# The modulation product with its weights as the stationary operand and two columns of conditions as the moving one

## The chip, the cores and the metric

The kernel runs on one core of one Trainium2 chip. The metric is the device time of one execution in microseconds (us). Three runs of the kernel before gave 1486.37, 1487.2 and 1495.71 us; the median is 1487.2 us.

## The reference, cut to what matters

The program is one inference step with two layers over 128 context tokens and 1024 latent tokens. Each layer begins with a modulation: a conditioning vector (one for the latent tokens, one for the context tokens) goes through SiLU and through a linear map, and gives a shift, a scale and a gate of 1024 values each.

```
mod = jax.nn.silu(cond) @ w_mod + b_mod               # w_mod: (1024, 3072) per layer, float32
shift, scale, gate = jnp.split(mod, 3, axis=-1)
h = _rmsnorm(x, g_pre) * (1.0 + scale[:, None, :]) + shift[:, None, :]
z = h @ w_in                                          # feeds attention, a gating MLP and a DeltaNet
...
return x + gate[:, None, :] * _rmsnorm(mix, g_post)   # mix = concatenated branches @ w_out
```

So the product has two rows of conditions, 1024 inputs and 3072 outputs, and its weights are 12 MB per layer. The scale and the shift are wanted by all that follows in their layer; the gate is wanted only by the layer's end.

## The kernel before

Tokens are in nine tiles of 128 (t = 0 to 7 latent, t = 8 context). A normalised tile is transposed on TensorE, scaled and shifted per feature, and split into two float16 halves, X (`make_h`, L275 to L291). Every projection of X (`proj_tok`, L165 to L171) is three float16 products per 128 inputs.

The order of the program is this. In the **prologue** (L1081 to L1102) the scale and the shift of layer 0 are made (parts 1 and 0 of `mod`, four `next` calls, L1087), then nine tiles are loaded, normalised and turned into X. Both scale and shift are in the tile `AB`; nothing of X can be made before it. Then, for each layer, `merge` (L1104) interleaves a chain (the DeltaNet) with a filler (the gating MLP, then attention) by estimated costs that the generators yield. The attention generator calls `next(other)` once after each tile of heads (L1018); `other` is the rest of the modulations: the gate of layer 0 (part 2) and all three parts of layer 1. At last `out_layer` projects back, makes the X of the next layer, and takes the gate from DRAM (`gg_d`).

The instructions are put in their order on each engine ahead of time by a scheduler of the framework; each engine then runs its own list in that order and waits where an operand is missing. SyncE (SP) issues nearly all DMAs, those of the attention's transposes too (`turn`), from one list.

`mod` (L210 to L259) takes 512 output columns at a time. Four loads of 512 KB bring the weights: 256 inputs x 512 columns each, in runs of 2 KB (L245). In the prologue they have 16 buffers of their own (`wm`); later they share two staging buffers (`st`) with the loads of the projection weights. The conditions are the stationary operand: the tile `csp` has 8 blocks of 32 columns, of which two hold conditions and 30 hold zeros. The four matmuls of four input blocks write to four groups of 32 partitions, so the result is in four partial sums on 128 partitions (L249). They are copied to SBUF (L251), and `finish` adds the four and transposes at once by products with a selection matrix `selc` (L227, for scale and shift: stationary are 128x128 blocks of the copy, moving the two columns of `selc`), then adds the bias. For the gate (L220) the sums stay as rows, and bias and `g_post` are loaded as rows by two small DMAs (L217, L218).

In the profile one float32 matmul of this kind shows as two records of weight load and two of matmul: 96 matmuls of L249 are 192 records, 32 of L227 are 64.

Of the kernel before, what the change touches and what calls it, by code (L numbers as in the profile page):

```python
# [11 lines left out]
F32 = mybir.dt.float32  # L12
# [34 lines left out]
def hybrid_trunk(  # L47
# [145 lines left out]
    def silu_cond(mp_):  # L193
# [10 lines left out]
        csp = mp_.tile([128, 8, 32], F32, name="csp")  # L204
        G.memset(csp, 0.0)
        V.scalar_tensor_tensor(csp[:, :, 0:2].transpose([0, 2, 1]), th.rearrange("p (c k) -> p c k", c=2), 1.0,
# [3 lines left out]
    def mod(l, vt, mp_, csp, AB, wmp=None):  # L210
        mt = [mp_.tile([128, 8, 2], F32, tag=f"mt{i}", name=nm("mt")) for i in range(2)]

        def finish(part, cb, mp):
            f0 = 4 * (cb % 2)
            if part == 2:
                rows = stg.tile([128, 4, 256], F32, tag="st", name=nm("gr")).rearrange("p a b -> p (a b)")[0:2].rearrange("p (a c) -> p a c", a=2)
                dma(rows[:, 0], b_mod[l, 512 * cb:512 * cb + 512].partition_broadcast(2))  # L217
                dma(rows[:, 1], g_post[l, 128 * f0:128 * f0 + 512].partition_broadcast(2))  # L218
                pm = bank("o", 1)
                T.matmul(pm[0:2, :], selc, mp, start=True, stop=True)  # L220
                V.tensor_tensor(rows[:, 0], pm[0:2, :], rows[:, 0], op=ALU.add)
                V.tensor_tensor(rows[:, 0], rows[:, 0], rows[:, 1], op=ALU.mult)
                dma(gg_d[l][:, 128 * f0:128 * f0 + 512], rows[:, 0])
                return
            pm = bank("o", 1)
            for b in range(4):
                T.matmul(pm[:, 2 * b:2 * b + 2], mp[:, 128 * b:128 * b + 128], selc, start=True, stop=True)  # L227
            V.tensor_tensor(mt[part][:, f0:f0 + 4], pm[:, 0:8].rearrange("p (f c) -> p f c", c=2),
                            bc(vt[:, 16 + 8 * part + f0:20 + 8 * part + f0], 2, 2), op=ALU.add)
            if cb % 2 and part == 1:  # L230
                V.scalar_tensor_tensor(AB[:, 0], mt[1], 1.0, bc(vt[:, 0:8], 2, 2), op0=ALU.add, op1=ALU.mult)
            elif cb % 2:
                V.tensor_copy(AB[:, 1], mt[0])

        todo = []
        for part in (1, 0, 2):
            for cb in (2 * part, 2 * part + 1):
                ps = psp()
                for k2 in range(4):
                    if wmp is not None and part < 2:  # L240
                        st = wmp.tile([128, 4, 256], F32, tag="wm", name=nm("wm"), bufs=16)
                    else:
                        st = stg.tile([128, 4, 256], F32, tag="st", name=nm("st"))
                    s = st.rearrange("p a b -> p (a b)").rearrange("p (k c) -> p k c", k=2)
# [5 lines left out]
                mp = mp_.tile([128, 512], F32, tag="mp", name=nm("mp"), bufs=2 if PIPE else 1)  # L250
                (V.tensor_copy if wmp is not None and part < 2 else S_.copy)(mp, ps)  # L251
                todo.append((part, cb, mp))
                if len(todo) > PIPE:
                    finish(*todo.pop(0))
# [1000 lines left out]
```

## Time and profile before

| | |
|---|---|
| time of the profiled execution | 1490.02 us |
| its span | 1487.9 us |
| median of three runs | 1487.2 us |
| busy share of the span: TensorE matmul, weight load | 88%, 68% |
| VectorE, ScalarE, GpSimd | 65%, 44%, 44% |
| mean granted TensorE clock | 0.945 of full |

A busy matmul engine is not one at its peak: matmuls are pipelined, and a record lasts longer than the distance to the next one. The cost of a stream of matmuls is read from the distances of starts. The granted clock has two levels, 1.0 (2.4 GHz) and 0.5 (1.2 GHz); a value between is a mean over both.

### The profile page before, as it was taken

Reading aid. Unit: us, or ns where it says so; the run is one execution under the profiler, and the core shown is the slowest. Engines: PE = TensorE matmul, PEld = TensorE weight load, DVE = VectorE, ACT = ScalarE, POOL = GpSimd, SP = SyncE. Lnnn points to the kernel's source line nnn. Section 1 sums busy time; section 2 is a strip of 40 time slices with the busy share of each in tenths; the row PEclk is TensorE's granted clock in tenths of the full one; section 3 lists DMA queues with packets and bytes.
Section 4 is the critical chain, followed back from the end, with each engine's and each line's share of the span. In section 5 each row is a group of like instructions: output and inputs, shape, how many; then the busy total and the mean of one; then the engine's idle time right before and its main releaser. Section 6 shows DMA issues by size and latency. Waiting matters only on the chain.

```text
span 1487.9 us, 37881 instructions
## 1 busy us (share of the span) xinstructions
PE 1311.8 (88%) x15191; PEld 1004.7 (68%) x15191; DVE 960.6 (65%) x2302; ACT 657.9 (44%) x1483; POOL 649.8 (44%) x890
## 2 busy tenths in 40 slices
PE   6899988899989699969998998889898769987997
PEld 2665566476668587758896655668676658865786
DVE  2865689986465684664446677797966375776333
ACT  2733545624465414742334344442567322765211
POOL 0751256624375423762223433553568512667200
PEclk9999999998999888989999998899999889998999
DMA  9331034727774225775342211332476111776553
GB/s 362 107 90 41 23 98 129 150 88 184 159 163 114 40 59 111 122 167 160 128 132 76 59 36 58 95 82 59 81 133 111 37 44 46 146 110 138 155 177 107
DMA packets 301563, 162.90 MB, mean 109 GB/s; under 512 B 212623, under 2 KB 277939, under 8 KB 301387
## 3 DMA queue, kind: packets, MB, share of 16 engines
q1 hardware_dynamic: 301261, 160.45, 44.2%
q8 instruction: 119, 1.95, 0.6%
q14 instruction: 58, 0.47, 0.1%
q10 hardware_dynamic: 125, 0.04, 0.0%
HBM read 95.78 MB, written 24.28 MB: 81 GB/s over the span
## 4 chain that ended last, share of the span: by engine, by line
PE 46%; DVE 18%; DMA 16%; issue 8%; POOL 7%; ACT 5%; SPq 1%; ACTq 0%; DVEq 0%; POOLq 0%
PE ps L170 13%; PE ps L1052 10%; PE ps L312 7%; DMA PT<-P 6%; DVE sv L500 2%; DVE sv L502 2%; POOL P L931 2%; PE ps L249 2%; PE ps L947 1%; DMA mix_d<-oc 1%; DMA st<-in_w_mod_dram 1%; PE ps L533 1%; DMA st<-in_w_in_dram 1%; PE ps L698 1%; PE ps L517 1%
## 5 line engine op out<-in xcount | busy, mean ns | idle before, releaser
L170 PEld LDWEIGHTS <-X 128*128 128x128 f16 x3888 | 351.8, 100 | 106.3 <-issue 42.0
L170 PE MATMUL ps<-wg,X 128*128 128x256 f16 x2592 | 330.5, 280 | 12.0 <-DVE wg L161 4.8
L931 POOL TENSOR_TENSOR P<-sS,P 128x512 f16<-128x512 f32 (+2 forms) x144 | 151.6, 1056 | 84.4 <-ACT sS L929 57.9
L1052 PEld LDWEIGHTS <-OTm 128*128 128x128 f16 x1728 | 169.7, 99 | 24.5 <-DMA OTm<-mix_d 2.6
L1052 PE MATMUL ps<-wo,OTm 128*128 128x256 f16 x1296 | 152.5, 277 | 1.9 <-DMA OTm<-mix_d 1.9
L312 PE MATMUL ps<-X,wg 128*128 128x512 f16 (+1 forms) x864 | 146.0, 328 | 1.8 <-ACT wg L160 1.4
L928 ACT ACTIVATE P<-sS,nmx 128x512 f16<-128x512 f32 (+2 forms) x144 | 94.3, 660 | 72.4 <-DVE nmx L926 46.5
L926 DVE CUSTOM_DVE_ANT_0 sS<-ps,am,nsk 128x512 f32<-128x512 f32 (+2 forms) x144 | 95.0, 669 | 42.1 <-PE ps L922 27.3
L312 PEld LDWEIGHTS <-wg 128*128 128x128 f16 x864 | 74.1, 99 | 68.5 <-ACT wg L160 1.8
L170 PE MATMUL ps<-wb,X 128*128 128x256 f16 x864 | 105.4, 284 | 11.6 <-ACT wb L160 6.6
L947 PE MATMUL ps<-Vt,PT 128*128 128x128 f16 (+1 forms) x992 | 71.4, 212 | 36.0 <-DMA PT<-P 34.9
L929 ACT ACTIVATE sS<-sS,nmx 128x512 f32<-128x512 f32 (+2 forms) x144 | 94.9, 659 | 4.6
L145 POOL TENSOR_TENSOR rs<-ms,mhalf 128x1 f32<-128x1 f32 x36 | 19.9, 554 | 168.9 <-DVE ms L1061 93.2
L947 PEld LDWEIGHTS <-PT 128*128 128x128 f16 x992 | 50.2, 100 | 55.0 <-DMA PT<-P 46.1
L319 DVE SCALAR_TENSOR_TENSOR y<-zT,cw,y 128x1156 f32<-128x1156 f32 x48 | 68.9, 1438 | 28.5 <-ACT y L317 27.9
L500 DVE TENSOR_TENSOR sv<-sv 128x31 f32<-128x31 f32 (+15 forms) x186 | 78.1, 420 | 3.8
L502 DVE TENSOR_TENSOR sv<-sv 128x31 f32<-128x31 f32 (+15 forms) x186 | 74.3, 399 | 4.0
L922 PE MATMUL ps<-KT,qT 128*128 128x128 f16 (+2 forms) x272 | 68.8, 267 | 0.0
L161 DVE SCALAR_TENSOR_TENSOR wg<-st,wg 128x1024 f16<-128x1024 f32 x44 | 55.4, 1268 | 19.4 <-ACT wg L160 19.2
L1055 ACT ACTIVATE sq<-ps 128x512 f32<-128x512 f32 x36 | 21.3, 594 | 100.8 <-PE ps L1052 57.8
L921 PE MATMUL ps<-KT,qT 128*128 128x128 f16 (+2 forms) x272 | 60.2, 268 | 6.0 <-DVE nmx L926 3.5
L160 ACT ACTIVATE wg<-st 128x1024 f16<-128x1024 f32 x44 | 45.3, 1055 | 43.3 <-DMA st<-in_w_in_dram 29.3
(271 smaller groups left out, 2818.0 us busy)
## 6 DMA issues: line engine op xcount, KB each, us to landing
st<-in_w_in_dram SPq DMA_DIRECT2D x40, 512.0 KB, 4.6
st<-in_w_mod_dram SPq DMA_DIRECT2D x32, 512.0 KB, 4.4
OTm<-mix_d SPq DMA_DIRECT2D x18, 512.0 KB, 4.9
wm<-in_w_mod_dram SPq DMA_DIRECT2D x16, 512.0 KB, 7.9
xt<-in_x_sample_dram SPq DMA_DIRECT2D x16, 512.0 KB, 11.8
st<-in_w_out_dram SPq DMA_DIRECT2D x16, 512.0 KB, 4.6
mix_d<-OTA SPq DMA_DIRECT2D x36, 128.0 KB, 3.3
xs<-xt SPq DMA_DIRECT2D x9, 512.0 KB
```

The source lines that it names most:

```text
L170: T.matmul(ps, X[:, t, k, a, :], wg[:, k, b, c0:c0 + n], start=(i == 0), stop=(i == 23))
L312: T.matmul(ps[:, 0:n], wg[:, k, b, 128 * hg:128 * hg + 128], X[:, t0:t1, k, a, :], start=(i == 0), stop=(i == 23))
L319: V.scalar_tensor_tensor(y, zT[:, tap:tap + 1156], cw[:, tap * 6 + ct:tap * 6 + ct + 1], y, op0=ALU.mult, op1=ALU.add)
L500: V.tensor_tensor(t3, m3[:, 0:m, m:m + 1].to_broadcast([128, m, w]), y3[:, m:m + 1, m:32].to_broadcast([128, m, w]), op=ALU.mult)
L502: V.tensor_tensor(y3[:, 0:m, m:32], y3[:, 0:m, m:32], t3, op=ALU.subtract)
L922: T.matmul(ps[:, cs], qT[:, h, :], Kl[:, kv, ks], start=False, stop=True)
L926: V.tensor_tensor_reduce(sS[:, 0:nk], ps[:, 0:nk], mk, -0.125, nsk[:, hh:hh + 1], ALU.add, ALU.min, accum_out=nmx[:, h:h + 1])
L928: S_.activation(P16[:, 0:nk], sS[:, 0:nk], AF.Exp, bias=nmx[:, h:h + 1], scale=-1.0)
L929: S_.activation(sS[:, 0:nk], sS[:, 0:nk], AF.Exp, bias=nmx[:, h:h + 1], scale=-1.0, accum_out=sm[:, h:h + 1])
L931: G.tensor_tensor(P16[:, nk:2 * nk], sS[:, 0:nk], P16[:, 0:nk], op=ALU.subtract)
L947: T.matmul(pops[:, 128 * h:128 * h + n], PT[:, a * nb + j, :], Vt[:, blist[j], kv].rearrange("p s d -> p (s d)")[:, 0:n], start=(i == 0), ...
L1052: T.matmul(ps[:, 256 * i:256 * i + 256], OTm[:, k, a, :], w[:, k, b, :], start=(n == 0), stop=(n == 23))
```

## The change

`csp` is now 128x8x2, without zeros. A new function `block(part, f, ws)` makes 128 outputs at once: eight matmuls, over eight blocks of 128 inputs, with a 128x128 block of the weights as the stationary operand and `csp[:, k, :]`, two columns, as the moving one. They are added up in one of the three `psp` banks, which the projections use too. The result is features by conditions already: ScalarE adds the bias of scale and shift on its way out of PSUM (128x2), VectorE adds the bias of the gate and multiplies by `g_post`. The copy, the products with `selc` and the small loads are gone; the gate is turned into rows by one transpose per layer. In the prologue the loads stay as they were. Elsewhere a load of 512 KB now brings all 1024 inputs of 128 columns, in runs of 512 B, and one `next` makes two blocks from two loads, where it made 512 columns from four; the 8 calls that found work are now 16, of 18 places. The cost yielded to the interleaving was 3.5 for each of 8 calls, and is 1.8 for each of 16.

```
-        csp = mp_.tile([128, 8, 32], F32, name="csp")
-        G.memset(csp, 0.0)
+        csp = mp_.tile([128, 8, 2], F32, name="csp")
...
+        def block(part, f, ws):
+            ps = psp()
+            for k in range(8):
+                T.matmul(ps[:, 0:2], ws[k], csp[:, k, :], start=(k == 0), stop=(k == 7))
+            bias = vt[:, 16 + 8 * part + f:17 + 8 * part + f]
             if part == 2:
...
+                V.tensor_scalar(mt[2][:, f, :], ps[:, 0:2], bias, vt[:, 8 + f:9 + f], op0=ALU.add, op1=ALU.mult)
+            else:
+                S_.activation(mt[part][:, f, :], ps[:, 0:2], AF.Identity, bias=bias)
+
+        def finish(part):
+            if part == 2:
                 pm = bank("o", 1)
...
+                T.transpose(pm[0:16, 0:128], mt[2].rearrange("p f c -> p (f c)"), ident)
+                rows = mp_.tile([16, 128], F32, tag="gr", name=nm("gr"))
+                V.tensor_copy(rows, pm[0:16, 0:128])
+                dma(gg_d[l].rearrange("c (f q) -> f c q", q=128), rows)
...
         for part in (1, 0, 2):
-            for cb in (2 * part, 2 * part + 1):
-                ps = psp()
-                for k2 in range(4):
...
-                    dma(s, w_mod[l, 256 * k2:256 * k2 + 256, 512 * cb:512 * cb + 512].rearrange("(k p) c -> p k c", p=128))
-                    for kk in range(2):
-                        k = 2 * k2 + kk
-                        j = k % 4
-                        T.matmul(ps[32 * j:32 * j + 32, :], csp[:, k, :], s[:, kk, :], start=(k < 4), stop=(k >= 4))
...
+            if wmp is not None and part < 2:
+                for cb in range(2):
+                    ws = [None] * 8
+                    for k2 in range(4):
+                        st = wmp.tile([128, 2, 512], F32, tag="wm", name=nm("wm"), bufs=16)
+                        dma(st, w_mod[l, 256 * k2:256 * k2 + 256, 1024 * part + 512 * cb:1024 * part + 512 * cb + 512]
+                            .rearrange("(k p) c -> p k c", p=128))
+                        ws[2 * k2], ws[2 * k2 + 1] = st[:, 0], st[:, 1]
+                    for b in range(4):
+                        block(part, 4 * cb + b, [w[:, 128 * b:128 * b + 128] for w in ws])
...
+                    yield 3.6
+                continue
+            for f in range(8):
+                st = stg.tile([128, 4, 256], F32, tag="st", name=nm("st"))
+                s = st.rearrange("p a b -> p (a b)").rearrange("p (k c) -> p k c", k=8)
+                dma(s, w_mod[l, :, 1024 * part + 128 * f:1024 * part + 128 * f + 128].rearrange("(k p) c -> p k c", p=128))
+                block(part, f, [s[:, k, :] for k in range(8)])
...
+                if f % 2:
+                    yield 1.8
```

How the change moves instructions is shown at three places; a number behind a name is that of a buffer.

TensorE in the prologue, before: the first 512 columns and their `finish` (`wm` are the weight tiles, `csp` the conditions, the moving operand stands first).

```order
L249 MATMUL ps_137<-wm_138,csp 32x512 x2
L249 MATMUL ps_137<-wm_142,csp 32x512 x2
L249 MATMUL ps_137<-wm_146,csp 32x512 x2
L249 MATMUL ps_137<-wm_150,csp 32x512 x2
L227 MATMUL ps_156<-selc,mp_154 128x2 x4
```

The same place in the changed kernel (line numbers are its own).

```order
L216 MATMUL ps_145<-csp,wm_137 128x2 x2
L216 MATMUL ps_155<-csp,wm_137 128x2 x2
L216 MATMUL ps_165<-csp,wm_137 128x2 x2
L216 MATMUL ps_145<-csp,wm_139 128x2 x2
L216 MATMUL ps_155<-csp,wm_139 128x2 x2
L216 MATMUL ps_165<-csp,wm_139 128x2 x2
L216 MATMUL ps_145<-csp,wm_141 128x2 x2
L216 MATMUL ps_155<-csp,wm_141 128x2 x2
L216 MATMUL ps_165<-csp,wm_141 128x2 x2
```

Three blocks run side by side as the weight tiles come in, in three banks; the fourth follows when a bank is free. In all there are 16 blocks, 128 such matmuls, with one other matmul (the transpose of the bias vectors) among them, ahead of the first transpose of a token tile.

ScalarE in the prologue, before: squares for the norms (L265), a conversion of projection weights (L160) and, sixth, the first use of `AB` (L286).

```order
L265 ACTIVATE sq_241,ss_242<-xt_239 128x1024
L265 ACTIVATE sq_251,ss_252<-xt_249 128x1024
L160 ACTIVATE wg_259<-st_260 128x4x256
L265 ACTIVATE sq_270,ss_271<-xt_268 128x1024
L265 ACTIVATE sq_303,ss_304<-xt_301 128x1024
L286 ACTIVATE hf_278<-ps_279,AB_125 128x128 x2
```

The same place in the changed kernel; L221 takes a block out of its bank.

```order
L160 ACTIVATE wg_351<-st_356 128x4x256
L221 ACTIVATE mt_134<-ps_252,vt_122 128x2
L221 ACTIVATE mt_134<-ps_262,vt_122 128x2
L160 ACTIVATE wg_1370<-st_1371 128x4x256
L221 ACTIVATE mt_134<-ps_272,vt_122 128x2
L160 ACTIVATE wg_1370<-st_1375 128x4x256
L221 ACTIVATE mt_134<-ps_290,vt_122 128x2
L221 ACTIVATE mt_134<-ps_300,vt_122 128x2
L221 ACTIVATE mt_134<-ps_310,vt_122 128x2
L221 ACTIVATE mt_134<-ps_320,vt_122 128x2
L264 ACTIVATE sq_395,ss_396<-xt_393 128x1024
L285 ACTIVATE hf_370<-ps_371,AB_124 128x128 x2
```

The blocks' way out of PSUM now stands among conversions of projection weights. Of the four conversions of the prologue, one stood ahead of the first use of `AB` before, and all four do now.

SyncE in the attention of layer 0, before (`PT` and `qT` are transposes that the heads wait for, `gr` the rows of the gate).

```order
L933 DMA_TRANSPOSE PT_3299<-P_448_3294 128x2x128
L217 DMA gr_3345<-in_b_mod_dram 2x512
L218 DMA gr_3345<-in_g_post_dram 2x512
L245 DMA st_3617<-in_w_mod_dram 128x2x512
L889 DMA rt_4242<-in_rope_dram 128x128
L933 DMA_TRANSPOSE PT_3310<-P_452_3305 128x2x128
L933 DMA_TRANSPOSE PT_3321<-P_456_3316 128x2x128
L245 DMA st_3621<-in_w_mod_dram 128x2x512
L899 DMA_TRANSPOSE qT_3464<-ql_3461 128x4x128
L933 DMA_TRANSPOSE PT_3545<-P_488_3540 128x6x128
L933 DMA_TRANSPOSE PT_3562<-P_492_3557 128x6x128
L245 DMA st_3625<-in_w_mod_dram 128x2x512
```

The same place in the changed kernel.

```order
L253 DMA st_3703<-in_w_mod_dram 128x8x128
L898 DMA_TRANSPOSE qT_3317<-ql_3314 128x4x128
L253 DMA st_3715<-in_w_mod_dram 128x8x128
L932 DMA_TRANSPOSE PT_3380<-P_449_3375 128x2x128
L932 DMA_TRANSPOSE PT_3391<-P_453_3386 128x2x128
L932 DMA_TRANSPOSE PT_3402<-P_457_3397 128x2x128
L932 DMA_TRANSPOSE PT_3413<-P_461_3408 128x2x128
L888 DMA rt_3982<-in_rope_dram 128x128
L253 DMA st_3907<-in_w_mod_dram 128x8x128
L932 DMA_TRANSPOSE PT_3634<-P_489_3629 128x6x128
L898 DMA_TRANSPOSE qT_3553<-ql_3550 128x4x128
L932 DMA_TRANSPOSE PT_3649<-P_493_3644 128x6x128
```

Of each `next` four loads through two buffers stood before among the transposes; now two loads stand there, and the small ones of the gate are gone.

## Rows read from the trace of the kernel before

**Rows 1.** Page, parts 1 and 4: engines; the chain that ended last, by engine.

```profile
PE 1311.8 (88%) x15191; PEld 1004.7 (68%) x15191; DVE 960.6 (65%) x2302; ACT 657.9 (44%) x1483; POOL 649.8 (44%) x890
PE 46%; DVE 18%; DMA 16%; issue 8%; POOL 7%; ACT 5%; SPq 1%; ACTq 0%; DVEq 0%; POOLq 0%
```

**Rows 2.** Busy us by stretch; columns named in the first row.

```profile
core 0: us, PE busy (x) PEld busy (x) DVE busy (x) ACT busy (x) POOL busy (x), PEclk, DMA share, GB/s
5.00:30.00 25.00, 19.77 (x98) 6.55 (x99) 4.96 (x15) 2.30 (x4) 0.55 (x1) 1.00 1.05 392
33.00:75.00 42.00, 34.06 (x272) 27.84 (x273) 35.40 (x84) 33.16 (x68) 28.99 (x34) 0.91 0.41 137
225.00:450.00 225.00, 202.61 (x2295) 138.88 (x2293) 169.82 (x439) 112.91 (x275) 116.54 (x164) 0.95 0.63 147
450.00:675.00 225.00, 190.10 (x2844) 157.88 (x2842) 141.72 (x383) 104.11 (x246) 109.77 (x164) 0.90 0.50 107
```

**Rows 3.** Timeline of the prologue: start us, us, what, [idle before it].

```profile
5.53 5.30 PE L249 MATMUL ps<-wm,csp 128*32 128x512 f32 x16 [2.50 <-DMA wm<-in_w_mod_dram]
...
11.62 0.97 PEld L227 LDWEIGHTS ps<-selc,mp 128*128 128x128 f32 x8 [1.91 <-DVE mp L251]
...
12.61 0.14 PEld L249 LDWEIGHTS ps<-wm,csp 128*32 128x32 f32 x2
...
27.62 1.05 PE L227 MATMUL ps<-selc,mp 128*128 128x2 f32 x8 [0.79 <-DVE mp L251]
...
29.78 0.17 DVE L233 COPY AB<-mt 128x16 f32<-128x16 f32 x1
...
33.33 1.68 DVE L288 TENSOR_SCALAR hf<-ps,AB 128x128 f32<-128x128 f32 x5
...
47.09 1.05 ACT L160 ACTIVATE wg<-st 128x1024 f16<-128x1024 f32 x1
```

**Rows 4.** Timeline of two streams of small matmuls and what followed one.

```profile
77.81 4.34 PE L170 MATMUL ps<-wab,X 128*128 128x16 f16 x167
...
358.42 4.34 PE L517 MATMUL ps<-sv,NA 32*32 32x32 f32 x128
362.69 1.87 PE L227 MATMUL ps<-selc,mp 128*128 128x2 f32 x8
364.48 1.92 PE L249 MATMUL ps<-st,csp 128*32 128x512 f32 x4
```

**Rows 5.** Stretches of these streams, matmul engine alone: busy, PEclk, DMA share, GB/s.

```profile
75.30:81.80 6.50, 6.50 (x225) 1.00 0.19 50
81.90:85.00 3.10, 3.10 (x54) 0.50 0.88 271
...
361.90:368.70 6.80, 6.80 (x42) 0.52 0.20 52
```

**Rows 6.** Groups by line and shape: busy us, mean ns, idle before, releaser.

```profile
L249 PE MATMUL ps<-st,csp 128*32 128x512 f32 x128 | 36.4, 633 | 5.8 <-DMA st<-in_w_mod_dram 5.8
...
L220 PE MATMUL ps<-mp,selc 128*2 128x512 f32 x8 | 4.1, 592 | 0.2 <-ACT mp L251 0.2
...
L161 DVE SCALAR_TENSOR_TENSOR wg<-st,wg 128x1024 f16<-128x1024 f32 x44 | 55.4, 1268 | 19.4 <-ACT wg L160 19.2
...
L958 ACT ACTIVATE es<-es 128x4 f32<-128x4 f32 x36 | 7.0, 194 | 0.2
```

**Rows 7.** Stretch 225 to 450, L227 alone: matmul, weight load, PEclk, DMA.

```profile
225.00:450.00 225.00, 4.98 (x32) 4.69 (x32) 0.95 0.63 147
```

**Rows 8.** The chain between 225 and 460, shares by line.

```profile
by line: PE ps L170 13.2%; PE ps L249 9.7%; DMA st<-in_w_mod_dram 9.0%; issue 8.6%; DVE sv L500 6.6%; DVE sv L502 5.9%; DMA PT<-P 4.1%; DVE sS L926 2.5%; PE ps L947 2.3%; PE ps L533 2.0%; DMA st<-in_w_in_dram 2.0%; PE ps L517 1.8%; PE ps L9
```

**Rows 9.** SP's waits: for whom, total us, times, longest.

```profile
SPq L245 <- PE ps L249: 21.3, 12, 6.7
```

**Rows 10.** DMA issues: KB each, median us to landing.

```profile
st<-in_w_mod_dram SPq DMA_DIRECT2D x32, 512.0 KB, 4.4
...
st<-in_w_in_dram SPq DMA_DIRECT2D x16, 256.0 KB, 3.1
```

More of the change, by code (lines that the diff above doesn't have):

```diff
@@ L203, in silu_cond @@
         V.tensor_scalar(ct, ct, 0.5, None, op0=ALU.mult)
[L204 to L206 removed]
+        csp = mp_.tile([128, 8, 2], F32, name="csp")
+        V.scalar_tensor_tensor(csp.transpose([0, 2, 1]), th.rearrange("p (c k) -> p c k", c=2), 1.0,
                                ct.rearrange("p (c k) -> p c k", c=2), op0=ALU.add, op1=ALU.mult)
@@ L210, in mod @@
     def mod(l, vt, mp_, csp, AB, wmp=None):
-        mt = [mp_.tile([128, 8, 2], F32, tag=f"mt{i}", name=nm("mt")) for i in range(2)]
-        def finish(part, cb, mp):
-            f0 = 4 * (cb % 2)
-            if part == 2:
-                rows = stg.tile([128, 4, 256], F32, tag="st", name=nm("gr")).rearrange("p a b -> p (a b)")[0:2].rearrange("p (a c) -> p a c", a=2)
-                dma(rows[:, 0], b_mod[l, 512 * cb:512 * cb + 512].partition_broadcast(2))
-                dma(rows[:, 1], g_post[l, 128 * f0:128 * f0 + 512].partition_broadcast(2))
-                pm = bank("o", 1)
[L220 to L230, printed above, removed]
@@ new lines, in mod @@
+        mt = [mp_.tile([128, 8, 2], F32, tag=f"mt{i}", name=nm("mt")) for i in range(3)]
+        def block(part, f, ws):
[3 more added lines that the diff above has]
+            bias = vt[:, 16 + 8 * part + f:17 + 8 * part + f]
+            if part == 2:
+                V.tensor_scalar(mt[2][:, f, :], ps[:, 0:2], bias, vt[:, 8 + f:9 + f], op0=ALU.add, op1=ALU.mult)
+            else:
+                S_.activation(mt[part][:, f, :], ps[:, 0:2], AF.Identity, bias=bias)
@@ L233, in finish @@
                 V.tensor_copy(AB[:, 1], mt[0])
-        todo = []
         for part in (1, 0, 2):
-            for cb in (2 * part, 2 * part + 1):
-                ps = psp()
-                for k2 in range(4):
[L240 to L244, printed above, removed]
-                    dma(s, w_mod[l, 256 * k2:256 * k2 + 256, 512 * cb:512 * cb + 512].rearrange("(k p) c -> p k c", p=128))
-                    for kk in range(2):
-                        k = 2 * k2 + kk
-                        j = k % 4
-                        T.matmul(ps[32 * j:32 * j + 32, :], csp[:, k, :], s[:, kk, :], start=(k < 4), stop=(k >= 4))
[L250 to L254, printed above, removed]
-                if (part, cb) in ((0, 1), (2, 5)):
-                    for x in todo:
-                        finish(*x)
-                    todo = []
-                yield 1
@@ new lines, in mod @@
+            if wmp is not None and part < 2:
[8 more added lines that the diff above has]
+                        block(part, 4 * cb + b, [w[:, 128 * b:128 * b + 128] for w in ws])
+                    if cb:
+                        finish(part)
+                    yield 3.6
+                continue
@@ new lines, in mod @@
+            for f in range(8):
[3 more added lines that the diff above has]
+                block(part, f, [s[:, k, :] for k in range(8)])
+                if f == 7:
+                    finish(part)
+                if f % 2:
+                    yield 1.8
@@ L1017, in attention @@
                             yield from heads(p2, prev, *ready.pop(0))
-                            if next(other, None) is not None:
-                                yield 3.5
+                            got = next(other, None)
+                            if got is not None:
+                                yield got
                     while pend:
```

3 lines of the change are left out of this document (2 added, 1 removed).

## The prediction, written before the changed kernel was run

> **What bounds the kernel now.** I read the page first, for the engines and the chain. TensorE is the busiest engine and holds nearly half of the chain that ended last [rows 1]. A change that gives or takes TensorE time therefore counts wherever TensorE is what the rest waits for, and there are two such places for the modulation.
>
> The first is the prologue. The stretch 5 to 30 us is bound by loads: 392 GB/s with the DMA engines fully busy, TensorE at 19.8 of 25 us [rows 2]. A weight tile of 512 KB comes each 1.34 us (0.524 MB over 392 GB/s), and TensorE follows it. The last product with `selc` starts at 27.62, the finished shift is in `AB` at 29.78 + 0.17 = 29.95, and its first use starts at 33.33 [rows 3]. From there to 75 the nine tiles are made, with VectorE busy 35.4 of 42 us [rows 2].
>
> The second is the attention of layer 0, from about 225 on, where the other 8 x 512 columns are made. Between 225 and 450 TensorE is busy 202.6 of 225 us, and 190.1 in the next 225 [rows 2]. The chain there gives L249 9.7% of 235 us = 22.8 us, and the waits for its weight loads 9.0% = 21 us [rows 8].
>
> **The price of a block.** The trace of before has the very instruction of the new blocks, a float32 128x128 stationary operand with two moving columns: L227. Eight records (four matmuls) at 11.62 are followed by the next weight load at 12.61 [rows 3], so a record takes 0.99/8 = 0.124 us, and a block of 16 records 1.98 us. The distance is that of the weight loads, which lie back to back. At the lower clock the same eight records start at 362.69 and the next matmul at 364.48 [rows 4], 1.79 us: 0.224 per record, 3.58 us per block.
>
> At 0.124, 48 blocks (16 in the prologue, 32 in the attention) cost 95 us. What they replace: in the attention L249 36.4 and L220 4.1 [rows 6] and L227 5.0 [rows 7], together 45.5 us; there 32 blocks cost 63.4. The zeros of the padded operand were cheap, since four partial products ran side by side on four groups of partitions; a weight load of 128 columns for two moving ones is dear.
>
> **Which clock the stream has.** In the prologue the 16 blocks are one stream of 256 records, with nothing wide among them. Two streams of small matmuls in the trace kept the engine fully busy and lost the clock. One with 16 moving columns and dense weight loads [rows 4] fills most of 75.3 to 81.8 at 1.00, and from 81.9 it is 0.50; the other, 128 records of 32x32, begins at 358.4, and 361.9 to 368.7 has 0.52, though TensorE is busy throughout [rows 5]. The matmuls of 512 columns in 5 to 30, with gaps, kept 1.00 [rows 2]. So I take the new stream to lose the clock about 5 us after its start, between the 3.5 and the 6.6 us of the two.
>
> **The sum, prologue.** The stream starts at 5.53 as before [rows 3]. It is no longer fed too slowly: three blocks side by side need 12 records x 0.124 = 1.49 us per weight tile, more than the 1.34 of its load. At 10.5, 20 of the 128 matmuls are done (0.248 each); the other 108 at 0.447 take 48.3 us, so it ends at 58.8 (57.5 to 60.0 for a loss at 12.1 or at 9.0). With the way out on ScalarE (nearest row, 128x4: 0.194 [rows 6]) and the copy, 0.17, the first use starts at about 59.6, 26.3 us later than 33.33. Some of it is caught up. By then all token tiles have landed and four conversions are done, three of which lay behind 33.33: 3 x 1.27 = 3.8 us of VectorE [rows 6]. VectorE also waits 42 - 35.4 = 6.6 us in that stretch. The catch-up lies between 0 and 10.4; I take 6, past the middle, since the loads no longer hold anything up while the chains between engines do. Prologue: **+20.3**, bounds +14 to +27.
>
> **The sum, attention.** TensorE has 63.4 - 45.5 = +17.9 at full clock. One of the four L227 groups in this stretch ran at the lower one [rows 4], so I take a quarter of the blocks at 3.58: 8 x 1.60 = +12.8, together +30.7 (bounds +17.9 and, all blocks low, +69). On the path lies the share that L249 has now, 22.8/36.4 = 0.6: +18.4. Against it stands the wait for the weights. A call issues two loads into two free buffers where four went through two, so the 5.8 us of TensorE's waits for them [rows 6], and SP's waits for L249, 21.3 us [rows 9] with the transposes queued behind, become less. I take 4. Attention: **+14.4**.
>
> Loads in runs of 512 B: the nearest row is 256 KB of projection weights in such runs, 3.1 us to landing, against 4.4 for 512 KB in runs of 2 KB [rows 10]; 512 KB then takes between 4.4 and 6.2. They are issued a call ahead, so I cost them at nothing; without that cover it is up to 32 x 1.8 = 58 us of landing time, 0.6 of it on the path. Of the 32 blocks' ways out, 16 are on ScalarE, 3.1 us, and 16 on VectorE about as much, on engines with half and a quarter of the stretch free [rows 2]: nothing. A block holds one of the three banks that the projections use; that is in the bounds.
>
> Together +34.7: 1490.0 + 34.7 = 1524.7 for an execution like the profiled one, which is 2.8 us above the median of the runs. Against the median: **1522 us**.
>
> **The rivals.**
>
> *The stream keeps its pace*: the clock holds, or the weight loads don't go with it. The stream would end at 5.5 + 31.7 = 37.2. But on ScalarE the blocks' ways out stand behind conversions whose loads come late: the third conversion starts at 47.09 now [rows 3], and the thirteenth block's way out stands behind the fourth. So the first use lies between 38 and 50, +5 to +16; at the middle, with 2 caught up, +8. The attention gives 17.9 x 0.6 - 4 = +7. Time 1487.2 + 15 = 1502. The two lost clocks [rows 5] and 1.79 us against 0.99 [rows 3, 4] speak against it. Chance 0.2. The Trainium skill, "TensorE: Matmul & The Clock Gate", section "LDWEIGHTS (loading the stationary operand)", has such a rule: a load takes its columns over 1.2 ns, at any clock. By that, 256 loads of 128 columns are an estimated 27.3 us and the stream ends at 32.9; the trace agrees at the full clock (0.124 against 0.107), and not at the lower (0.224).
>
> *The attention runs low too*: wide projections between the blocks don't hold the clock, and all 32 blocks cost 3.58. Then 69 x 0.6 = +41.4, with the prologue +62: 1549. For it speaks the 0.90 of the second stretch [rows 2]; against it that in the order long runs of 256-column products stand between blocks. Chance 0.15.
>
> *Faster: the load queue was the bound.* If the 21 us that the chain gives to the waits for weights [rows 8] go, the +17.9 fit into TensorE's idle 22.4 + 34.9 us of the two stretches [rows 2], and the clock holds in the prologue with the 5 us caught up, the time is 1487.2 - 21 = 1466. It decides at a stream that ends before about 38 us; each us later costs one. Chance 0.05.
>
> *Covered*: as before, but the waits move to other transfers. Time 1487 + 0 to 5: 1490. Chance 0.05.
>
> **How the numbers follow.** The forecast has 0.55 (1508 to 1538). About 1% is what a measurement of this kernel tells from no change, so 1472 to 1502 is no change: all of the last rival and a third of the first, 0.12. Faster 0.04, slower 0.84. The range goes from 1497, inside the first rival, to 1553, past the second: 1497 to 1553 leaves out the covered and the faster case, the low end of the first rival and a tail above.
>
> **What would show it.** The profile of the changed kernel should have: the clock at 0.50 from about 10 us to beyond 55; starts of the block records 0.22 us apart there; the copy of the shift into `AB` near 59 instead of 29.95; the dense stretch after the tiles (wide products of the DeltaNet's features) some 20 us later; L216 with 32 x 2 to 3.6 us between 225 and 675, spread over both halves of the attention, and TensorE's waits for `w_mod` below 5.8. I am wrong if the copy into `AB` is before 50, or if the attention of layer 0 takes no longer than before.

## The result, and the profile after

The changed kernel takes **1556.1 us** (median of four runs, 1545.2 to 1564.1) against 1488.6 for the kernel before on the same chip: 1.044 times as long (95% interval 1.040 to 1.048). The forecast was 1522 with a range up to 1553: the sign was right, the size was not. The profiled execution took 1564.1 us, its span is 1562.3; so there are 74.4 us to account for between two spans. It is the slowest of the four executions, 8 us above their median; lengths read from its trace can be a few us long for that.

The page, parts 1 and 4 of the changed kernel:

```profile
PE 1400.2 (90%) x15697; PEld 1139.6 (73%) x15697; DVE 954.3 (61%) x2300; ACT 658.3 (42%) x1507; POOL 647.2 (41%) x889
PE 51%; DVE 20%; DMA 9%; issue 8%; POOL 6%; ACT 5%; SPq 0%; ACTq 0%; DVEq 0%; POOLq 0%
```

Against [rows 1] TensorE has 88 us more and the weight loads 135; the other engines have what they had. DMA has shrunk in the chain from 16% to 9%: by line, the waits for the attention's weights of the modulation are gone from it and those for `PT` have gone from 6% to 4%, and TensorE has filled their place and more.

The prologue, timeline of TensorE and of VectorE (start us, us, what, [idle before it]):

```profile
5.75 9.94 PE L216 MATMUL ps<-csp,wm 128*128 128x2 f32 x46 [2.69 <-DMA wm<-in_w_mod_dram]
...
16.54 44.54 PE L216 MATMUL ps<-csp,wm 128*128 128x2 f32 x208 [0.32 <-ACT mt L221]
...
60.94 1.95 PE L280 MATMUL ps<-ident,xt 128*128 128x128 f32 x8
...
61.41 0.17 DVE L233 COPY AB<-mt 128x16 f32<-128x16 f32 x1 [11.40 <-ACT mt L221]
62.07 1.26 DVE L287 TENSOR_SCALAR hf<-ps,AB 128x128 f32<-128x128 f32 x3 [0.49 <-PE ps L280]
```

Of the 46 records the starts are 9.94/46 = 0.216 us apart, of the 208 it is 44.54/208 = 0.214: the lower pace from the first record on, not from 10 us.

The kernel before starts at that level too. Its products of 512 columns in two stretches of the prologue, 5 to 9.4 us and 12 to 30 (ns min/median/max, first and last start):

```profile
L249 PE MATMUL ps<-wm,csp x12: 1031/1061/1062, 5.5 to 9.0; 128*32 128x512 f32 x12
...
L249 PE MATMUL ps<-wm,csp x48: 592/593/617, 12.6 to 26.2; 128*32 128x512 f32 x48
```

The list of granted clocks in each trace begins with a rise to 1.0: at 10.1 us in the kernel before, and at 66.8 in the changed one, where the stream has ended (61) and wide products run. Ahead of its first entry the list is empty, and a view then prints 1.00, as in 5 to 30 us [rows 2]. So the new stream didn't lose the higher clock, it never got it. The shift is in `AB` at 61.6 where 59 was forecast, and the first use is at 62.07 instead of 33.33 [rows 3], **+28.7**. The first wide product of the DeltaNet's features starts at 111.6 instead of 82.5, +29.1: nothing was caught up on the way.

Busy time by stretch (columns as in [rows 2]):

```profile
5.00:30.00 25.00, 23.94 (x112) 23.88 (x113) 0.39 (x2) 2.50 (x8) 0.11 (x1) 1.00 1.04 390
...
225.00:450.00 225.00, 206.23 (x2275) 178.27 (x2272) 173.07 (x445) 104.91 (x263) 113.78 (x166) 0.87 0.48 108
450.00:675.00 225.00, 202.11 (x2550) 174.38 (x2546) 118.87 (x324) 90.39 (x223) 91.95 (x135) 0.83 0.48 111
```

In the attention of layer 0 the granted clock is 0.87 and 0.83 where it was 0.95 and 0.90. Groups by line and shape, of the blocks in the attention and in the prologue:

```profile
L216 PE MATMUL ps<-csp,st 128*128 128x2 f32 x512 | 73.9, 268 | 0.0
L216 PE MATMUL ps<-csp,wm 128*128 128x2 f32 x256 | 55.0, 352 | 3.0 <-DMA wm<-in_w_mod_dram 2.7 <-ACT mt L221 0.3
```

and the loads of the attention (KB each, median us to landing):

```profile
st<-in_w_mod_dram SPq DMA_DIRECT2D x32, 512.0 KB, 4.5
```

32 blocks took 73.9 us, 2.31 each, between the two prices forecast (1.98 and 3.58). TensorE's waits for these weights, 5.8 us before [rows 6], are gone. A load of 512 KB in runs of 512 B lands in 4.5 us, as fast as in runs of 2 KB (4.4, [rows 10]).

Where the 74.4 us arose, by landmarks in both traces: +33.1 up to the first product of query and key of layer 0 (247.2, now 280.3); **+38.5** from there to the first feature product of layer 1 (813.6, now 885.2); +2.8 in all that follows. The feature products of layer 1, before and after (first and last start behind the durations; the weight load of the first starts 0.1 us ahead of it):

```profile
L312 PE MATMUL ps<-X,wg x432: 218/379/389, 813.7 to 903.5; 128*128 128x512 f16 x97, 128*128 128x128 f16 x47
...
L311 PE MATMUL ps<-X,wg x432: 219/379/389, 885.3 to 975.6; 128*128 128x512 f16 x97, 128*128 128x128 f16 x47
```


For the attention I cut out the same piece of the program in both traces, from the first to the last product of query and key of layer 0. Before, then after, then the blocks of the changed kernel alone:

```profile
247.20:640.80 393.60, 347.36 (x4565) 259.94 (x4566) 268.64 (x707) 190.33 (x458) 194.19 (x275) 0.94 0.55 120
```

```profile
280.40:718.60 438.20, 402.37 (x4952) 347.07 (x4951) 264.66 (x717) 188.31 (x468) 194.05 (x278) 0.84 0.49 108
...
280.40:718.60 438.20, 71.36 (x490) 71.50 (x490) 0.84 0.49 108
```

The piece is 44.6 us longer. The modulation has 71.4 us of TensorE where L249, L220 and L227 had 35.4 + 4.1 + 5.0 = 44.4: **+27.0**, about what was forecast for it. But the *other* TensorE work of the piece grew too: 402.4 - 71.4 = 331.0 against 347.4 - 44.4 = 302.9, **+28.1**. Some of it is other content: the order puts 4462 such records between the two landmarks where it put 4405, and 57 more at the old mean of 0.069 us are an estimated 4 us; the rest, 24, is the same kind of records taking longer. TensorE's idle time shrank from 46.2 to 35.8, -10.4. The middle term was nowhere in my sum.

### The profile page after: what moved, and what is told of

Read it like the earlier page. It is cut to its first block, busy times and chain, and to the rows that moved or that the text cites. A ratio compares the mean times of both kernels' runs of the same rounds, so it can differ in the third digit from the quotient of the medians.

```text
span 1562.3 us, 38893 instructions
## 1 busy us (share of the span) xinstructions
PE 1400.2 (90%) x15697; PEld 1139.6 (73%) x15697; DVE 954.3 (61%) x2300; ACT 658.3 (42%) x1507; POOL 647.2 (41%) x889
## 4 chain that ended last, share of the span: by engine, by line
PE 51%; DVE 20%; DMA 9%; issue 8%; POOL 6%; ACT 5%; SPq 0%; ACTq 0%; DVEq 0%; POOLq 0%
PE ps L170 13%; PE ps L1052 10%; PE ps L311 7%; PE ps L216 5%; DMA PT<-P 4%; DVE sv L501 3%; DVE sv L499 3%; PE ps L697 2%; POOL P L930 2%; PE ps L946 1%; DVE sS L925 1%; DMA st<-in_w_in_dram 1%; PE ps L532 1%; PE ps L516 1%; DVE wg L161 1%
## 5 line engine op out<-in xcount | busy, mean ns | idle before, releaser
L170 PEld LDWEIGHTS <-X 128*128 128x128 f16 x3888 | 357.6, 102 | 86.7 <-issue 22.1
L170 PE MATMUL ps<-wg,X 128*128 128x256 f16 x2592 | 338.5, 286 | 10.5 <-DVE wg L161 5.5
L946 PE MATMUL ps<-Vt,PT 128*128 128x128 f16 (+1 forms) x992 | 74.7, 218 | 24.1 <-DMA PT<-P 23.6
L946 PEld LDWEIGHTS <-PT 128*128 128x128 f16 x992 | 55.2, 104 | 40.3 <-DMA PT<-P 31.8
L161 DVE SCALAR_TENSOR_TENSOR wg<-st,wg 128x1024 f16<-128x1024 f32 x44 | 56.2, 1287 | 36.6 <-ACT wg L160 36.5
L216 PEld LDWEIGHTS ps<-csp,st 128*128 128x128 f32 x512 | 74.0, 222 | 2.1 <-issue 0.3
L216 PE MATMUL ps<-csp,st 128*128 128x2 f32 x512 | 73.9, 268 | 0.0
L921 PE MATMUL ps<-KT,qT 128*128 128x128 f16 (+2 forms) x272 | 72.2, 279 | 0.0
L920 PE MATMUL ps<-KT,qT 128*128 128x128 f16 (+2 forms) x272 | 63.6, 280 | 6.1 <-DVE OTA L980 3.1
```

The source lines that it names most:

```text
L170: T.matmul(ps, X[:, t, k, a, :], wg[:, k, b, c0:c0 + n], start=(i == 0), stop=(i == 23))
L216: T.matmul(ps[:, 0:2], ws[k], csp[:, k, :], start=(k == 0), stop=(k == 7))
L921: T.matmul(ps[:, cs], qT[:, h, :], Kl[:, kv, ks], start=False, stop=True)
L946: T.matmul(pops[:, 128 * h:128 * h + n], PT[:, a * nb + j, :], Vt[:, blist[j], kv].rearrange("p s d -> p (s d)")[:, 0:n], start=(i == 0), ...
```

## The experiments

Two theories stood against each other. **Clock**: two moving columns behind a weight load of 128 lose TensorE's clock, for the blocks and for what runs beside them. **Form**: the 512-byte runs, the banks, or 16 calls spread over both halves cost the attention its time. A third, **order**, came up on the way: the framework sets every engine's list anew after any edit. All times are medians; the interval is that of the ratio to the kernel before, run beside it (1489 to 1493 us). "The piece" is the one above.

### One half of the change at a time

e1_prologue_new: the new blocks for parts 1 and 0 of layer 0 only; e2_attention_new: only for the other 32 blocks.

> The new blocks in the prologue only (parts 1 and 0 of layer 0); the 32 blocks of the attention are in the old form. Theory 1 (the stream of 256 weight loads runs at the lower pace from its first record, the tiles behind it start late, and nothing is caught up because VectorE paces the nine tiles): the copy into AB stays near 61 us, the first use near 62, and the kernel takes 1488.6 + 26 to 30 = 1515 to 1519 us; from first to last QK of layer 0 393.6 us as before, within 6. My forecast's own term (6 us are caught up): 1488.6 + 20 = 1508 to 1510. Rival (prologue and attention are coupled: the late start shifts which loads meet in the attention): the stretch from first to last QK grows by over 15 us here too, and the time is above 1525.

> The new blocks in the attention only; the prologue is in the old form. Theory 1 (the blocks cost TensorE 27 us more than what they replace, and the clock that they lose slows the other TensorE work of the stretch by another 28, less 10 of idle time): first to last QK of layer 0 takes 393.6 + 38 to 46 us, TensorE's busy time there outside the modulation is 325 to 336 us instead of 303, and the kernel takes 1488.6 + 36 to 44 = 1525 to 1533 us. My forecast's term for the attention alone (+14.4): 1503. Rival (coupling: the loss in the attention comes with the late start): under 1515, with the other TensorE work at 303 to 312.

e1: 1521.1 us (1.016 to 1.025), e2: 1553.4 us (1.039 to 1.047). In e1 the copy into `AB` starts at 61.15, features start at 111.5, and the attention is as before (piece 387.6 us, clock 0.94; from its first product of query and key to the features of layer 1 566.5 us, where the kernel before takes 566.4): the prologue costs its 29 us, with nothing caught up, and a late start alone costs the attention nothing. e2 is 20 us above what I had expected. Its piece takes 443.5 us, 407.0 of it TensorE, 72.2 modulation, so other work 334.8. But 28 + 61 are 89 and not 67: the halves don't add, and e2's own attention (+50 to the features of layer 1) is worse than that of the changed kernel (+38.5). Neither theory has a term for that.

### A wide moving side

e3_wide, and e8_w32 with 32 in place of 128:

```
-                T.matmul(ps[:, 0:2], ws[k], csp[:, k, :], ...)
+                T.matmul(ps[:, 0:128].rearrange("p (a b) -> p a b", b=2), ws[k], bc(csp[:, k, 0:2], 1, 64), ...)
```

> The changed kernel with one edit: the moving operand of each block has 128 columns, the two conditions repeated 64 times (read with stride zero), and the first two columns of the product are used. Stationary operands, loads, order and ways out are the same; only what TensorE streams behind each weight load differs. Theory 1 (two moving columns behind a weight load of 128 lose the clock; with 128 moving columns it is held): records 0.12 to 0.13 us apart in the prologue, the copy into AB at 37 to 46 us, the blocks of the attention near 64 us of TensorE, the other TensorE work from first to last QK back to 300 to 310 us, that stretch 393.6 + 9 to 19 us, and the kernel at 1500 to 1520 us. Rival (the 512-byte runs of the loads, the banks or the order of 16 calls cost the attention its time): the stretch stays at 393.6 + 38 or more and the kernel above 1530. If the clock is lost because of the dense weight loads and not of the narrow moving side, the prologue stays at 61 or later and the time at 1556 or above.

> As the run with 128 moving columns, with 32. The records stay bound by their weight loads, so only what TensorE streams differs. If the clock follows the streamed columns by degree: records in the prologue at 0.2155 us, the copy into AB near 61 us, the other TensorE work of the attention at 315 to 331 us, and the kernel at 1530 to 1560 us. Rival (anything above a handful of columns keeps the clock): copy into AB at 37 to 42 us and the kernel at 1490 to 1502 us.

e3 took **1495.5 us** (1.000 to 1.005), e8 1550.7 (1.036 to 1.044). In both, `csp` has 32 columns per block again, of which the products read two. Timeline of TensorE in the prologue, e3 (its first line is that of the window 5 to 9.5 us) and then e8:

```profile
5.57 4.18 PE L219 MATMUL ps<-csp,wm 128*128 128x128 f32 x18 [2.53 <-DMA wm<-in_w_mod_dram]
...
13.67 23.49 PE L219 MATMUL ps<-csp,wm 128*128 128x128 f32 x208 [0.36 <-ACT mt L227]
37.00 1.04 PE L340 MATMUL ps<-ident,xt 128*128 128x128 f32 x8
```

```profile
16.27 44.59 PE L219 MATMUL ps<-csp,wm 128*128 128x32 f32 x208 [0.27 <-ACT mt L227]
```

The same 208 records with the same weight loads: 0.113 us apart with 128 columns, 0.214 with 32, as with 2. So the pace isn't the weight load's own, it is the engine's; with 64 times the columns to stream the same blocks are done in half the time. e3 starts at the lower pace too (4.18 us for its first 18 records), its list of clocks begins with a rise at 9.8 us, and e8's at 69.4. In the piece of e3 (then its blocks alone) the other work is 365.7 - 68.0 = 297.7 us:

```profile
247.20:648.80 401.60, 365.67 (x4975) 314.82 (x4976) 268.75 (x721) 188.60 (x469) 195.02 (x280) 0.95 0.53 118
...
247.20:648.80 401.60, 68.01 (x490) 61.26 (x490) 0.95 0.53 118
```

That looks like the end of the story, and it is not: by the clock theory 24 us more of modulation on TensorE should still have cost some, and e3 lost nothing up to the features of layer 1 (812.7 against 813.6). e8 lies between in the attention: its blocks take 67.8 us in a piece of 411.0, the other work 311.0, at a granted clock of 0.89.

### The old form with other loads

All with the conditions stationary. e4_old_runs: tiles of 8 row blocks x 128 columns, in runs of 512 B. e5_four: 4 x 256, runs of 1 KB. e7_split: the old matmuls on a tile whose loads go in runs of 512 B.

> The old form everywhere (the padded conditions stationary), but in the attention each weight tile holds 128 columns of all eight row blocks, loaded in runs of 512 bytes as in the changed kernel, and feeds eight matmuls of 128 moving columns, four side by side. Theory 1 (loads in short runs cost nothing here; the weight loads of 128 columns do): 1488.6 - 15 to + 3 us, since four products instead of two run side by side. Rival (the short runs are what the attention lost): 1488.6 + 20 or more, with the waits for w_mod on TensorE above 15 us.

> The old form everywhere, with another cut of the attention's weight tiles: four row blocks of 256 columns instead of two of 512, in runs of 1 KB, so that four products of 256 columns can run side by side on the four groups of partitions once one tile has landed. If TensorE time in the attention is worth what the old path share said (0.6) and the clock is kept: the modulation takes 26 to 34 us of TensorE between first and last QK of layer 0 instead of 44.4, and the kernel 1480 to 1490 us. Rival (what slowed the run with tiles of 128 columns was the clock, which fewer streamed columns at a time cost): 1500 to 1515 us at a granted clock of 0.93 or less. Rival (it was the short runs): about half of that run's loss, 1500 to 1508, with TensorE's waits for w_mod at 10 to 16 us.

> The kernel before with one edit: each weight tile of the attention is laid out so that its load goes in runs of 512 bytes, as two transfers of 256 KB; the matmuls (512 moving columns, two side by side) are the same. If the short runs are what cost the run with tiles of 128 columns its 25 us: 1510 to 1520 us, TensorE's waits for w_mod above 20 us. If it was the shape of its matmuls (128 columns, four side by side) that cost the clock: 1487 to 1497 us, granted clock 0.94 to 0.95.

They took 1517.2 (1.014 to 1.023), 1527.4 (1.020 to 1.028) and 1524.9 us (1.018 to 1.025). All are slower, also those that give TensorE less to do: e4's modulation takes 30.9 us in its piece instead of 44.4, and the piece is 393.8 us long, as before. e4's loss comes later, after the modulation is done (442 us): the last product of the DeltaNet's scan (L577 in the kernel before) starts at 712.2 instead of 697.0. I had expected -15 to +3. By its numbers the rival came true: over 1508, and 25.9 us of TensorE's waits for these weights. e5 has 17.0 us of such waits and a clock of 0.92, and takes longer than any of its theories said; e7 has 19.3 us of waits, about what was named for short runs, and takes 5 us more. So these three leave short runs open as a cause in the old form; f3 below takes the runs away.

e6_calls4: the changed kernel with four blocks per call, in 8 calls.

> The changed kernel with four blocks in a call instead of two, so that the 32 blocks of the attention come in 8 calls, in its first half, where the old form had them, as denser streams of 64 records. Theory 1 (the narrow blocks lose the clock wherever they stand, the longer the stream the more): blocks at 75 to 95 us of TensorE in that stretch, the other TensorE work there at 320 or more, the kernel between 1545 and 1575 us. Rival (what cost the attention its time is that blocks now stand in its second half, where nothing hides them): 1520 to 1540 us.

1601.6 us (1.068 to 1.077), slower than either expected. The spread over both halves was no fault. Denser streams make the blocks dearer, 88.6 us in the piece instead of 71.4, but the piece is only 2 us longer (440.3). Between the two profiled executions lie 29 us, of which 18 arise in layer 1, where no block is left (the last starts at 531 us): the blocks don't explain them.

### Keeping the order

The framework sorts the instructions by estimated durations, and the new blocks have other estimates than the old ones: of the 14,929 matmul records outside the modulation in the trace of e3, 3904 write or read other tiles than the record at the same place in the changed kernel. To keep the order, these runs change the operands after the lists are made (f1 has 10 such records against the changed kernel):

```
+            for x, i in enumerate(ins):
...
+                m, w = i.ins
+                ins[x] = copy.replace(i, ins=[cols(m, [[0, 64], [1, 2]]), w], outs=[cols(i.outs[0], [[2, 64], [1, 2]])])
```

f1_pin128 does this to the changed kernel; f4_pin_att128 only to its attention; f2_e3order_2 goes back from 128 to 2 columns in the order of e3; f3_e7order_long gives e7 its 2-KB runs back.

> The changed kernel with each engine's list of instructions exactly as it is (the order is set first), and only then the moving operand of all 48 blocks widened from 2 to 128 columns (the two conditions repeated). So nothing differs but what TensorE streams behind the same weight loads. Theory 1 (the narrow moving side costs the clock, and the clock costs the time): copy into AB at 37 to 46 us, the other TensorE work from first to last QK of layer 0 back from 331 to 295 to 310 us, the kernel at 1490 to 1510 us. Rival (the framework sets the order anew after every edit, and the attention lost its time to a worse order): the prologue gains its 24 us, the attention nothing: 1525 to 1540 us.

> The converse: the order of the run with 128 columns (whose time was 1495), kept as it is, and then the moving operand narrowed to two columns. Theory 1: 1540 to 1565 us, with the prologue's copy into AB at 61 and the other TensorE work of the attention at 320 to 335 us. Rival (order): only the prologue's 24 us come, 1515 to 1525, with the other TensorE work at 298 to 306.

> The changed kernel in its own order, with 128 moving columns in the 32 blocks of the attention and two in the 16 of the prologue. By theory 1 and with costs that add: the prologue keeps its copy into AB at 61 us and its 29 us, the attention loses nothing; so the time lies 22 to 28 us above the run with 128 columns everywhere in this order, at 1515 to 1530 us. Rival (the late prologue is caught up once the attention has its clock): within 10 us of that run.

> The run whose loads of w_mod were cut into runs of 512 bytes (1525 us), with its order kept, and then tiles and loads laid out in runs of 2 KB, as in the kernel before; transfers are still two of 256 KB per tile. If the short runs cost it its time: 1487 to 1500 us, TensorE's waits for w_mod below 10 us instead of 19. If it is the order (which every edit sets anew) or the doubled number of transfers: 1515 to 1527 us.

| us | 2 columns | 128 columns |
|---|---|---|
| order of the changed kernel | 1556.1 | 1536.1 (f1) |
| order of e3 | 1545.2 (f2) | 1495.5 (e3) |

(Intervals: f1 1.025 to 1.037, f2 1.031 to 1.043.) f1 falls where the order theory put it and f2 where the clock theory did: each is half of it. The piece of f1, its blocks, and the same of f2:

```profile
268.60:692.60 424.00, 375.51 (x4950) 321.69 (x4951) 264.95 (x718) 188.03 (x468) 194.63 (x277) 0.92 0.51 112
...
268.60:692.60 424.00, 67.64 (x490) 60.99 (x490) 0.92 0.51 112
```

```profile
273.70:696.40 422.70, 394.79 (x4978) 340.23 (x4976) 268.81 (x721) 188.30 (x468) 195.16 (x279) 0.86 0.52 112
...
273.70:696.40 422.70, 72.40 (x490) 72.92 (x490) 0.86 0.52 112
```

| piece, us | length | modulation | other TensorE work | idle |
|---|---|---|---|---|
| before | 393.6 | 44.4 | 302.9 | 46.2 |
| changed | 438.2 | 71.4 | 331.0 | 35.8 |
| f1: same order, 128 columns | 424.0 | 67.6 | 307.9 | 48.5 |
| f2: order of e3, 2 columns | 422.7 | 72.4 | 322.4 | 27.9 |
| e3 | 401.6 | 68.0 | 297.7 | 35.9 |

At a fixed order the narrow blocks cost the *other* work 331.0 - 307.9 = 23.1 us in the one order and 322.4 - 297.7 = 24.7 in the other, and the blocks themselves only 3.7 and 4.4. Of these 27 and 29 us of TensorE, 14.2 and 21.1 show in the length. Only the streamed columns differ, and the granted clock goes with them (0.84 against 0.92, 0.86 against 0.95): that is the clock, shown. With the columns fixed, the order of the changed kernel is 424.0 - 401.6 = 22.4 us longer than that of e3 at 128 and 438.2 - 422.7 = 15.5 at two; part of it may be clock again, 0.92 against 0.95 at 128.

f4 took 1548.8 us (1.033 to 1.045): 12.7 above f1 and not 22 to 28, since f1's prologue isn't fast either: the first product of query and key starts at 268.6 us in f1 and at 279.6 in f4, and from there to the features of layer 1 both take 590 to 591 us. TensorE in the prologue of f1:

```profile
13.45 10.98 PE L216 MATMUL ps<-csp,wm 128*128 128x128 f32 x96 [0.35 <-ACT mt L221]
29.80 11.34 PE L216 MATMUL ps<-csp,wm 128*128 128x128 f32 x80 [5.36 <-ACT mt L221]
44.80 6.51 PE L216 MATMUL ps<-csp,wm 128*128 128x128 f32 x32 [3.66 <-ACT mt L221]
```

and ScalarE, for which it waits:

```profile
43.53 1.06 ACT L160 ACTIVATE wg<-st 128x1024 f16<-128x1024 f32 x1 [6.14 <-DMA st<-in_w_in_dram]
44.50 0.24 ACT L221 ACTIVATE mt<-ps,vt 128x2 f32<-128x2 f32 x1
46.38 1.06 ACT L160 ACTIVATE wg<-st 128x1024 f16<-128x1024 f32 x1 [1.63 <-DMA st<-in_w_in_dram]
47.34 0.40 ACT L221 ACTIVATE mt<-ps,vt 128x2 f32<-128x2 f32 x2
```

The 96 records are 0.114 us apart. Then the blocks' ways out stand in ScalarE's list behind conversions whose loads land late, the three banks are full, and TensorE waits; `AB` is copied at 51.6. In e3's order the ways out stand further ahead, and it is 37.5. This is what the first rival described; in the changed kernel the slow stream hid it.

f3 took 1517.5 us (1.014 to 1.028). TensorE still waits 18.3 us for these weights (e7: 19.3), so the long runs take next to none of the waits away, and the loss stands with them. The ratios to the kernel before are 1.0214 (e7) and 1.0208, the medians 7 us apart, and the intervals leave room for some 12 us either way. Whether e7 lost its time to its order or to its doubled number of transfers, which f3 keeps, is not separated.

### The order alone

g1_3p4 and g1_3p9 are the kernel before with one number changed, which only sorts the same instructions otherwise; g3_after_yield17 does that to the changed kernel (`yield 1.7`).

```
-                                yield 3.5
+                                yield 3.4
```

> The kernel before with one number changed: the cost that the attention's generator yields for a piece of modulation, 3.4 instead of 3.5. Every engine has the same instructions; the order differs from the layer-0 attention on. If the order alone is worth some 20 us (the kernel before stands in a good one): 1500 to 1520 us. Rival (the form costs, not the order): 1485 to 1497.

> As the run with 3.4, with 3.9, which moves more instructions (about a quarter of TensorE's stand at another place). Order: 1500 to 1525 us. Rival: 1485 to 1497.

> The changed kernel with 1.7 instead of 1.8 as the cost of two blocks: same instructions, another order in the attention. If the order is worth some 20 us either way: at least 8 us away from 1556, more likely below (1525 to 1548), since the order of the changed kernel was found to be a poor one. Rival (form): 1548 to 1562.

**1518.4 us** (1.014 to 1.023) and **1516.5 us** (1.012 to 1.021), with no instruction more or less; g3 1564.2 (1.043 to 1.053), as far from 1556 as I had said but on the other side, and with an interval that overlaps the changed kernel's, so no difference is shown there. The piece of g1_3p4 is as long as before:

```profile
247.50:641.50 394.00, 345.66 (x4477) 257.71 (x4478) 273.76 (x703) 189.13 (x456) 192.63 (x271) 0.94 0.55 120
```

but the scan's last product comes at 709.3 instead of 697.0, and the features of layer 1 start at 830.7 instead of 813.6. In g1_3p4:

```profile
L577 PE MATMUL ps<-vn,kd x288: 218/218/366, 392.0 to 709.3; 64*64 64x64 f32 x144
...
L312 PE MATMUL ps<-X,wg x432: 217/379/390, 830.9 to 922.2; 128*128 128x512 f16 x97, 128*128 128x128 f16 x47
```

The attention's last product of weights and values (L947) is in time, at 650.8 against 652.4; it is the DeltaNet's scan that is late, by 12 us. Another 12 us go in layer 1. Less of the higher clock goes with it: 2 x (1 - 0.931) x 1516.9 = 209 us of the span are at the lower clock, against 2 x (1 - 0.945) x 1487.9 = 164. How much of the loss that makes, and what in an order makes it good, I have not isolated.

g4_old_wide: old prologue, 128 columns in the attention.

> The prologue in the old form, and in the attention the new blocks with 128 moving columns, in the order that the framework gives it. With the clock kept: other TensorE work from first to last QK at 292 to 308 us. If its order is as good as that of the run with 128 columns everywhere: 1485 to 1497 us; if not, up to 25 more.

1498.8 us (1.002 to 1.007), other work in the piece 293.8. No version beats the kernel before.

## Why the prediction was wrong

- *Price of a block, and what it replaces*: held. 0.124 us per record at the full clock was measured as 0.113 to 0.114 (with 128 moving columns; no dense stream of two ran at it), 0.224 at the lower as 0.214 to 0.216; TensorE's modulation grew by 27.0 us in the piece where 30.7 was forecast, and the waits for the weights went away as said.
- *Clock in the prologue*: the lower level, as forecast, but by another way. I took the 1.00 of 5 to 30 us [rows 2] for a stream that starts at the full clock and loses it after 5 us. It starts at the lower level, as the kernel before and e3 do, and where theirs rose at about 10 us, that of the changed kernel did at 66.8. Copy into `AB` at 61.4 for a forecast of 59: near, since only 20 of 128 products were priced at the full clock. (The terms of that sum add up to a first use at 59.2, and it has 59.6.) The rival "the stream keeps its pace" is out for two columns, and its estimate by the Trainium skill with it: "TensorE: Matmul & The Clock Gate", section "LDWEIGHTS (loading the stationary operand)", gives a load its columns over 1.2 ns and names no clock; for 128 columns that is an estimated 0.107 us. The wide blocks of e3 agree (0.113), the narrow ones don't (0.214).
- *Catch-up of 6 us*: failed. +28.7 at the first use, +29.1 at the features. The work done ahead was real: four of six conversions (L161) are gone from VectorE's list between these two points. But its normalisations (L271, L270 after the change) take longer. Before (33.3 to 82.5), then after (62 to 111.6):

```profile
L161 DVE SCALAR_TENSOR_TENSOR wg<-st,wg 128x1024 f16<-128x1024 f32 x6 | 7.8, 1300 | 0.8 <-ACT wg L160 0.8
L271 DVE TENSOR_SCALAR xt<-xt,rs 128x1024 f32<-128x1024 f32 x7 | 6.4, 910 | 1.5 <-POOL rs L145 1.4
```

```profile
L161 DVE SCALAR_TENSOR_TENSOR wg<-st,wg 128x1024 f16<-128x1024 f32 x2 | 3.4, 1757 | 0.0
L270 DVE TENSOR_SCALAR xt<-xt,rs 128x1024 f32<-128x1024 f32 x6 | 8.1, 1344 | 3.2 <-POOL rs L145 3.2
```

  With some small instructions that are longer too, VectorE is busy for 43.0 of 49.6 us, and was for 42.1 of 49.2. Why they take longer is not isolated. e1 lost its 29 us in the same way. With the 4 us that came between the features and the attention, the prologue makes +33.1 for a forecast of 20.3, 13 of the 40 us by which the profiled execution went past the +34.7 of the forecast.
- *Attention, +14.4*: **the step that failed**, by 24 us. I multiplied the blocks' own extra time by the old path share, 0.6, and let everything else stand. Two things did not stand. The lost clock slows the neighbours: 23 to 25 us of TensorE at a fixed order, of which with the blocks' own 4 some 14 to 21 reach the end. And the order is set anew: with wide blocks (f1), from the first product of query and key to the features of layer 1, the changed kernel's order still takes 590.6 us where the kernel before takes 566.4. So the +38.5 are 14 that go with the narrow columns and 24 that remain with wide ones; e3 with the same work in another order takes 565.7, which makes these 24 a matter of order. Taken the other way round (f2 takes 586.3) it is 21 of clock and 19 of order (604.9 - 586.3): the two don't simply add, and each number is of one profiled execution. The two runs of the kernel before in other orders lost 17 and 13 in that stretch, and 24 to 26 in all, by order alone.
- *The attention runs low too* (1549) was the rival nearest in time, and its reason was at work only in part: the clock fell (0.84 for 0.94 in the piece), but the blocks cost 2.31 us and not 3.58, and what it cost lay in the work beside them and in the order. That it came near is luck.
- *Loads in runs of 512 B at nothing*: held. TensorE's idle time ahead of the blocks of the attention is 0.0 us, the loads land in 4.5, and e3 with the same loads is level with the kernel before.

## What to carry to other kernels

In this kernel a matmul that loads 128 columns of weights to stream two cost more than its own time: look at what the granted clock does to its neighbours, and price those too. Where a framework sorts the instructions, an edit is two changes, the edit and a new order; re-sort the old kernel by a trivial number and keep the order while the operands change, before you give a loss to the edit. A kernel that happens to stand in a good order looks better than any edit of it: here two copies of the old kernel, sorted otherwise, lost 24 to 26 us.

## What the runs showed of the hardware

- In a dense stream of float32 products with a 128x128 stationary operand, those with 128 moving columns ran twice as fast as those with 2 or 32 (0.113, 0.214 and 0.214 us per record): the granted clock rose at 9.8 us in the first, and in the others at 66.8 and 69.4, behind the stream. Four such products of two columns among wide ones ran at 0.124 us per record [rows 3].
- The granted clock reads 1.00 over the changed kernel's first 75 us, though its records were at the lower pace until 61, and the eight records of transposes behind them took 1.95 us, where those of e3 took 1.04. The list of clocks has its first entry at 66.8 us, and the view prints 1.00 ahead of it: there the pace had to be read from the distances of starts.
